# Low parts of 32 weight slabs by accumulating DMAs onto the negated rounded weights

## The chip, the cores and the metric

The kernel runs on one core of one Trainium2 chip, in one launch. The metric is the device time of that launch in microseconds (us), as a median of several executions. The engines of the core are TensorE (PE in the rows, with its weight loads as PEld), VectorE (DVE), ScalarE (ACT), GpSimd (POOL) and SyncE (SP), which here only issues DMAs.

## The reference, cut to what matters

One step of an encoder layer over 640 tokens (512 of a prompt, 128 of eight sample groups), width 1024:

```python
h = rmsnorm(x, norm_mix_g)
z = h @ w_in                      # query latent | kv latent | rotary key | GLU input | two gates
q = rmsnorm(c_q, q_norm_g) @ w_uq # then rotary, attention over cache and prompt -> attn_branch
u = u2[..., :C] * sigmoid(u2[..., C:])
conv_branch = silu(layernorm(depthwise_conv(u))) @ w_conv_out
x = x + (sigmoid(g_a) * attn_branch + sigmoid(g_c) * conv_branch) @ w_out
x = x + square(relu(rmsnorm(x) @ w_ff_up)) @ w_ff_down
x = x + sigmoid(rmsnorm(x) @ w_ple_gate) * (p_emb @ w_ple_proj)
```

All of it is float32. The products that this document is about are the query down-projection (`w_cq`), the query up-projection (`w_q`), the two gates (`w_gate`) and the projection of the convolution's branch (`w_conv_out`).

## The kernel before, in words

TensorE multiplies in float32r, a rounded form of float32. To keep the accuracy, each operand is split: a high part `hi` (the value rounded to float32r) and a low part `lo` (value minus `hi`). A product then has three terms, hi by hi, hi by lo and lo by hi, each for two halves of the 640 tokens: `mms` (L332) issues, for each block of 128 rows of the contraction, `wh*xh`, `wh*xl`, `wl*xh`, two matmuls each. So the low part of a weight slab is first read by the fifth matmul of its product. A product over 1024 rows has 48 matmuls, one over 768 rows (`w_q`) has 36.

Weights come as a stream of slabs (`jobs`, L224 to L254). `fetch` (L260) starts the load of the next slab into one of three buffers `raw` on SP's queue. `prep` (L269) takes a loaded slab, has ScalarE round it into `hi` (L287), and makes a function `low` that subtracts `hi` from `raw` into `lo` (L290), on VectorE, or on GpSimd for the slabs named in `POOL_SLABS` (L48: `w_gate` 0 to 7 and `w_q` 4 and 5). Then it calls `fetch` again. There are three buffers each for `hi` and `lo`. `slab` (L304) keeps three slabs ready, so the slab of product p+2 is prepared when the code comes to product p; its buffers are those of product p-1, and come free when TensorE has finished that product. `product` (L344) first runs the steps put down for the start, then issues some taps of the convolution, then `flush` (the `low` of the slab just prepared), then the matmuls, then the steps put down for after them.

The order of the instructions on each engine is the order of the code. Beside the products run: the convolution, three of its four channel tiles on VectorE (L485, the sums in PSUM), the fourth with multiplications on ScalarE (L501, L502) and additions on GpSimd (L510), two taps at most for each product; and short chains that make a norm's factor for each token. The one that matters here is that of the query latent, `chain("cbc")` (L744): for each of six products `cq`, ScalarE rounds the result (L363), VectorE makes its low part (L364), ScalarE squares it (L445), and GpSimd adds the squares (L446, `ssum_cq`). After the product `qr0` TensorE sums over partitions (L402, `ps_cbc`), VectorE scales (L641, L642), GpSimd takes the power (L643), VectorE multiplies (L644) and makes diagonal blocks (L419, `dg_cbc`), and after the product `qr1` TensorE spreads them (L395, `psb_cbc`). A like chain for the kv latent (`rkv`) stands earlier; between its steps VectorE has the rotary key (L699 to L702), whose multiplication waits for the load of `rope_k` (L695). That load is issued on SP behind the stores of the convolution's state (L624, L625), which go out in pieces of 120 bytes.

Products in order around the change: `kv0`, `kv1`, `kr`, `cq0` to `cq5`, `qr0`, `qr1`, `qn0` to `qn3` (the last six read `w_q` 0 to 5), `sc0` to `sc7` and `sa0` to `sa7` (`w_gate` 0 to 15), and eight products `co` on four slabs `w_conv_out`.

Of the kernel before, what the change touches and what calls it, by code (L numbers as in the profile page):

```python
# [14 lines left out]
P = 128  # L15
D = 1024
NP_ = 512          # prompt tokens
NB = 8             # sample batches
NQ = 16            # tokens per sample batch
NS = NB * NQ  # L20
T = NP_ + NS       # 640 columns: prompt tokens, then sample tokens (b, q)
# [6 lines left out]
C = 256            # latent width  # L28
QL = 768
CC = 512           # conv channels  # L30
# [9 lines left out]
# columns of the packed per-partition vectors  # L40
NT_RING = 9
SPLIT = 5  # the rows of the last product from here on by two groups of tokens: the norm of the first runs under the second
SO_LAG = 2.0
# taps of the convolution beside each product
# [3 lines left out]
POOL_SLABS = [f"w_gate_{i}" for i in range(8)] + ["w_q_4", "w_q_5"]  # L48
FFN_SLOPE, FFN_WAIT = 0.01, 0.2
POOL_LOW = (0, 1, 2, 3)  # of each four slabs of the lower product those whose second half Pool splits  # L50
# [7 lines left out]
NORM = ("DVE2", "DVE2", "ACT")  # of query tiles (3), (0, 1), (2): who divides by the sums of the softmax  # L58
# [4 lines left out]
SQ = ("M", "M", "M", "A")  # C11 C12 C21 C22: the square on the scalar engine alone, or the product on the vector engine  # L63
SQ2, START, SQ3 = "POOL", "POOL", "POOL"
UP_S = ("POOL", "POOL", "POOL", "DVE2")  # S1 S2 S3 S4
DN_S = ("POOL", "POOL", "POOL", "POOL")
DN_T = ("POOL", "DVE2", "POOL", "POOL")
UP_PS = (1, 0)  # the sums of weights in PSUM
# [4 lines left out]
FAST = (0, 1, 2, 3, 4, 5, 6)  # the chunks of the lower product by seven products  # L73
# the schedule of the attention: time between groups of samples, lag of the prompt, cost of a wait
# [6 lines left out]
class Slots:  # L81
    """Hands out tags of one-buffer slots; a freed slot goes to the back of the queue."""
# [17 lines left out]
class Plan:  # L100
    """A list schedule: operations with rough costs, issued in the order in which a model of the
    engines would start them. Engines, results waited for, and buffers taken and given back count."""
# [66 lines left out]
def encoder_step_kernel(ctx: ExitStack, tc: tile.TileContext, a: dict, o: dict):  # L169
# [7 lines left out]
    # PSUM by phase: two-bank tiles for the wide products (one of them for the sums of the  # L177
    # convolution), single banks for attention and what follows
# [81 lines left out]
    def fetch():  # L260
        """Starts the load of the next slab."""
        if pos[0] < len(jobs):
            src, cols, nm = jobs[pos[0]]
            pos[0] += 1
            raw = wraw.tile([P, 1024], F32, tag="raw", name=f"raw_{nm}")
            nc.sync.dma_start(raw[: src.shape[0], :cols], src)
            raws.append((raw, cols, nm))

    def prep():  # L269
# [4 lines left out]
        raw, cols, nm = raws.pop(0)  # L274
# [6 lines left out]
        if nm.startswith("cache_T"):  # L281
            # room for the new keys behind those of the cache
            hv, lv = (t.rearrange("p (c n) -> p c n", c=2)[:, :, :512] for t in (hi, lo))
            rv = raw.rearrange("p (c n) -> p c n", c=2)
        else:
            hv, lv, rv = hi[:, :cols], lo[:, :cols], raw[:, :cols]
        nc.scalar.activation(hv, rv, AF.Identity)  # L287

# [23 lines left out]
    # Each engine issues in the order of the code. Steps of a chain that wait for one another on  # L312
    # several engines are put between the products: `after` n products, or at the start of the nth next.
# [18 lines left out]
    def mms(ps, ws, xs, m=P, first=True, last=True):  # L332
        """ps[:m] += sum over k of w_k.T x_k with both operands split; ws: (hi, lo) blocks; xs: (hi, lo) [128, 640]."""
# [23 lines left out]
    def split(hi, lo, src, g=None):  # L357
        """hi + lo == src (times g) exactly, both in float32r."""
# [9 lines left out]
    def split_later(hi, lo, src, g=None):  # L368
        """split, the low part at the start of the next product."""
# [21 lines left out]
    def colsum(src, name):  # L391
        """Sum over partitions, on every partition."""
        ps = mm_ps(name)
        for s in range(2):
            nc.tensor.matmul(ps[:, s, :HT], ones, src[:, s * HT : (s + 1) * HT], start=True, stop=True)  # L395
        return ps

    def tok_sum(src, name):
        """Sum over partitions, tokens on partitions: [128, 5]."""
# [8 lines left out]
    def rstd(ssum, width, eps, name, which=0, out=None):  # L408
        """(ssum / width + eps) to the power, by token: [128, 5]."""
# [6 lines left out]
    def diag(r, name):  # L416
        """A column of tokens [128, 5] as five diagonal blocks; colsum makes it a row on every partition."""
# [13 lines left out]
    def sqsum(acc, src, first, name):  # L431
        """acc (+)= src * src."""
# [15 lines left out]
    def big(name):  # L448
        """[128, 8, 640] float32r pair as four slots."""
# [21 lines left out]
    def conv_ops():  # L471
        """The sums of the taps stay in PSUM: a multiply-add then leaves the port to GpSimd."""
# [22 lines left out]
    def conv_ops0():  # L495
        """The first channel tile: products on the scalar engine, sums on GpSimd."""
# [45 lines left out]
    # the first two slabs come in parts between the rows of x, so that the products start early  # L542
# [20 lines left out]
    # the clock of the tensor engine rises with use  # L563
# [64 lines left out]
    kv = Q.get([P, 4, T], "kv")  # raw 0:2, normalised 2:4  # L628
# [8 lines left out]
    def joint_rstd(ssum, width, name, scale, rc, rsq):  # L637
        """scale * rc * rsqrt(rc^2 * ssum / width + eps), by token: [128, 5]."""
# [8 lines left out]
    def chain(out, ssum, width, name, scale, then):  # L647
        """The row of joint_rstd by way of three products, then `then`."""
# [33 lines left out]
    def lat_new():  # L682
        """the new latents of the sample groups by token"""
# [30 lines left out]
    def rope_pair(xa, xb, n, name, out):  # L714
        """o1 = xa cos - xb sin, o2 = xb cos + xa sin; then out(o1, o2)."""
# [18 lines left out]
    cqA = [Q.get([P, 4, T], f"cq{i}", F32R) for i in range(3)]  # hi 0:4 | lo 0:4 | hi 4:6, lo 4:6  # L734
# [141 lines left out]
    krs = [t[:96, 2048:] for t in kTs]  # raw rotary keys of a group, three times  # L876
# [4 lines left out]
    # rotary parts, split and stacked: [hi hi lo] of the queries meets [hi lo hi] of the keys  # L881
# [65 lines left out]
    # slabs of the weight stream: k-th of the region takes the buffers of the (k - 3)rd  # L947
    slab_at, used = [], []

    def slab_op(key, hi_cost=0.95, lo_eng="DVE", lo_cost=1.14, raw_only=False):  # L950
        """Returns the index and the ops that complete the slab."""
# [30 lines left out]
    # keys and values of the prompt  # L982
# [54 lines left out]
    # absorbed queries of the sample groups  # L1037
    # the outputs of a group take the place of its queries
# [57 lines left out]
    # sample groups: scores, maximum, exponentials, transposes, values, back to latents on partitions  # L1096
# [3 lines left out]
    def group(b):  # L1100
# [14 lines left out]
        def key_new():  # L1115
            """the new keys of the group behind those of its cache"""
# [132 lines left out]
    # prompt: block-causal, query tiles of 128; a unit is a head with query tiles (3), (0, 1) or (2)  # L1249
    pair = {}  # L1250

    def unit(u, h, ts):
# [47 lines left out]
        # transposed blocks by key tile, the query tiles of one key tile side by side  # L1300
# [19 lines left out]
        def values():  # L1320
            """the outputs of a pair of heads share a bank"""
# [74 lines left out]
    # The channel mixer multiplies by one level of Strassen's method (Winograd's form): seven products  # L1396
    # of halves instead of eight. Rows in two halves by parity of their tile (B1x even, B2x odd), tokens
    # in two halves (Bx1, Bx2); of the operands B11, B21, B22, T1 = B12 - B11, T2 = B22 - T1,
    # T3 = B22 - B12, T4 = B21 - T2.
# [15 lines left out]
    def operand(i):  # L1415
        """Operand i as pairs (hi, lo) by pair of row tiles."""
# [11 lines left out]
    vrow = R.get([P, T], "vrow")  # mean(x^2) + eps of a token: r2 = 1 / v  # L1428
    ev2 = cols_[:, 4:9]  # eps v^2
# [22 lines left out]
    # the norm of the channel mixer by way of a column  # L1452
# [17 lines left out]
    def token_row(i, out, dep, key):  # L1470
        """A column of tokens as a row on every partition."""
# [27 lines left out]
    # the weight stream of the region  # L1499
    loads = []  # L1500

    def load(nm, key):
        """Starts the load of the next slab; its tile is in the box."""
# [28 lines left out]
    def take(cost, fn, deps, key):  # L1532
        """An op of the scalar engine that takes a pair of split buffers: they are taken in order."""
# [9 lines left out]
    def weights(nm, key):  # L1543
        """A slab for plain products, split; its pair of buffers is in the box."""
# [19 lines left out]
    # the values of the sample groups, from the outputs over the latents  # L1564
# [1238 lines left out]
```

## Time and profile before

| | us |
|---|---|
| median of 3 runs (1003.68 to 1004.9) | 1004.87 |
| span of the profiled execution | 1003.1 |
| TensorE busy in it | 977.9 |
| VectorE busy | 798.2 |
| ScalarE busy | 507.7 |
| GpSimd busy | 370.0 |

The profile is one execution; its span is 1.8 us below the median of the timed runs. Matmuls overlap one another: one takes some 0.31 us by its record, but in a product one starts every 0.147 us. A row of the timeline gives the start, the duration, the engine, the line, and what is written from what; in square brackets at its end stands how long the engine was idle before it and what ended that. Rows for several like instructions are merged (x2).

### The profile page before, as it was taken

The page shows a single profiled execution, that of the slowest core. Times are in us where ns is not written, and L with a number is a line of the kernel's source. Part 1 is how long each engine was busy: PE and PEld are TensorE (multiplying, and loading weights), DVE is VectorE, ACT ScalarE, POOL GpSimd, SP SyncE. Part 2 cuts the span into 40 slices and gives each one's busy share as a digit, 9 for nine tenths or more (in the row PEclk, how much of TensorE's full clock was granted, in tenths as well). Part 3 has the DMA queues.
Part 4 walks back from the last instruction along what each step waited for, and adds up shares of the span by engine and source line. Part 5 has one row for each costly group of instructions (what it writes and reads, how often), then busy time and mean ns, then how long its engine had stood idle before and what let it go on. Part 6 is the DMA issues. An engine that isn't in the chain of part 4 may idle for free.

```text
span 1003.1 us, 17048 instructions
## 1 busy us (share of the span) xinstructions
PE 977.9 (97%) x6570; PEld 941.1 (94%) x6570; DVE 798.2 (80%) x1417; ACT 507.7 (51%) x941; POOL 370.0 (37%) x270
## 2 busy tenths in 40 slices
PE   8999999999999999999999899999999999999996
PEld 8999989999999777799998799999999999999995
DVE  6596899995554787777888999999999999996445
ACT  7334544223443777635565445555455555645443
POOL 0354559322201433000329435454545454414011
PEclk9999999999999999999999999999999999999998
DMA  6329213312142343323312122223232222342203
GB/s 228 120 81 91 99 48 94 123 64 85 63 131 71 114 129 108 111 64 124 103 43 85 63 73 97 83 86 88 85 100 87 86 85 84 111 125 65 85 1 105
DMA packets 34705, 92.53 MB, mean 92 GB/s; under 512 B 8800, under 2 KB 11488, under 8 KB 34624
## 3 DMA queue, kind: packets, MB, share of 16 engines
q1 hardware_dynamic: 34480, 91.42, 30.7%
q8 instruction: 52, 0.85, 0.3%
q14 instruction: 29, 0.24, 0.1%
q10 hardware_dynamic: 144, 0.03, 0.0%
HBM read 86.12 MB, written 3.91 MB: 90 GB/s over the span
## 4 chain that ended last, share of the span: by engine, by line
PE 80%; DVE 12%; DMA 2%; ACT 2%; issue 2%; POOL 2%; SPq 0%; DVEq 0%; POOLq 0%; ACTq 0%
PE a L1909 10%; PE da L2176 9%; PE sa L342 6%; PE sc L342 6%; PE wo L1678 6%; PE b L1909 5%; PE db L2176 5%; PE pg L2472 3%; DVE cv L485 3%; PE ao L1615 3%; PE co L342 3%; PE pd L2292 3%; PE c L1909 2%; PE dc L2176 2%; PE pg L2551 2%; PE qn L342 2%
## 5 line engine op out<-in xcount | busy, mean ns | idle before, releaser
L2132 POOL TENSOR_TENSOR lo_B<-raw_down,hi_B 128x768 fp32r<-128x768 f32 x28 | 51.8, 1850 | 44.4 <-PE da L2176 21.1
L485 DVE SCALAR_TENSOR_TENSOR cv<-uP,keep,cv 128x512 f32<-128x512 f32 x87 | 65.6, 754 | 2.4
L2213 DVE TENSOR_TENSOR x<-da,x 128x320 f32<-128x320 f32 x112 | 53.7, 483 | 3.2 <-PE da L2176 0.9
L510 POOL TENSOR_TENSOR acc<-acc,tap 128x640 f32<-128x640 f32 x30 | 49.2, 1639 | 10.1 <-ACT tap L502 8.7
L2176 PE MATMUL da<-f,hi_B 128*128 128x320 f32 x224 | 50.2, 310 | 0.0
L2176 PE MATMUL da<-f,hi_A 128*128 128x320 f32 x224 | 49.6, 307 | 0.0
L2176 PE MATMUL db<-f,hi_A 128*128 128x320 f32 x224 | 49.6, 307 | 0.0
L1705 POOL TENSOR_TENSOR ssum<-ssum,sq 128x640 f32<-128x640 f32 x7 | 11.0, 1572 | 93.9 <-ACT sq L1702 93.9
L2113 POOL TENSOR_TENSOR raw_down<-raw_down 128x256 f32<-128x256 f32 x28 | 21.4, 763 | 60.5 <-DVE S L2105 60.1
L2125 ACT ACTIVATE hi_B<-raw_down 128x768 fp32r<-128x768 f32 x28 | 23.7, 848 | 31.4 <-PE a L1909 13.4
L1678 PE MATMUL wo<-mgl,hi_wo 128*128 128x320 f32 x128 | 39.4, 308 | 0.0
L1678 PE MATMUL wo<-mgh,hi_wo 128*128 128x320 f32 x128 | 39.1, 305 | 0.0
L1678 PE MATMUL wo<-mgh,lo_wo 128*128 128x320 f32 x128 | 39.0, 305 | 0.0
L2176 PEld LDWEIGHTS da<-f,hi_B 128*128 128x128 f32 x224 | 36.9, 187 | 0.7 <-DVE x L2213 0.2
L2176 PEld LDWEIGHTS db<-f,hi_A 128*128 128x128 f32 x224 | 37.1, 188 | 0.0
L2176 PEld LDWEIGHTS da<-f,hi_A 128*128 128x128 f32 x224 | 37.1, 188 | 0.0
L2125 ACT ACTIVATE hi_A<-S 128x512 fp32r<-128x512 f32 (+1 forms) x56 | 26.8, 479 | 17.4 <-DVE S L2119 17.4
L2176 PE MATMUL da<-f,lo_A 128*128 128x320 f32 x112 | 34.4, 307 | 0.8 <-DVE lo_A L2132 0.7
L2176 PE MATMUL db<-f,lo_A 128*128 128x320 f32 x112 | 34.2, 305 | 0.0
L2176 PE MATMUL da<-f,lo_B 128*128 128x320 f32 x112 | 34.2, 305 | 0.0
L2045 POOL TENSOR_TENSOR f<-y,f 128x640 fp32r<-128x640 f32 x7 | 11.7, 1673 | 59.7 <-ACT f L2038 59.7
L485 DVE SCALAR_TENSOR_TENSOR cv<-uS,keep,cv 128x128 f32<-128x128 f32 x87 | 31.0, 356 | 3.2
(686 smaller groups left out, 3785.5 us busy)
## 6 DMA issues: line engine op xcount, KB each, us to landing
raw_down<-in_w_down_dram SPq DMA_DIRECT2D x32, 512.0 KB, 3.6
raw_w_gate<-in_w_gate_dram SPq DMA_DIRECT2D x16, 512.0 KB, 3.5
raw_cache_T<-in_cache_T_dram SPq DMA_DIRECT2D x8, 512.0 KB, 3.6
raw_cache_V<-in_cache_V_dram SPq DMA_DIRECT2D x8, 512.0 KB, 3.5
raw_wo<-in_w_out_dram SPq DMA_DIRECT2D x8, 512.0 KB, 3.6
raw_pg<-in_w_pg_dram SPq DMA_DIRECT2D x8, 512.0 KB, 3.5
raw_w_glu<-in_w_glu_dram SPq DMA_DIRECT2D x6, 512.0 KB, 4.4
raw_w_cq<-in_w_cq_dram SPq DMA_DIRECT2D x6, 512.0 KB, 3.9
```

The costliest lines, as they stand in the source:

```text
L342: nc.tensor.matmul(ps[:m, s, :HT], w_, x_[:, s * HT : (s + 1) * HT], start=st_, stop=sp)
L485: nc.vector.scalar_tensor_tensor(out=outs[i] if j == W - 1 else sums[i], in0=src, scalar=wj, in1=sums[i], op0=ALU.mult, op1=ALU.add,)
L510: nc.gpsimd.tensor_tensor(out=acc[:, 0, :], in0=acc[:, 0, :], in1=t, op=ALU.add)
L1615: nc.tensor.matmul(ps[:, :HT], w_, x_[:, halves_[s]], start=k == 0 and n == 0, stop=k == 3 and n == 2)
L1678: nc.tensor.matmul(bx[s][:, :HT], w_, x_[:, n_], start=k == 0 and j == 0, stop=k == 7 and j == 2)
L1909: nc.tensor.matmul(bx[bank][:, :HT], w_, x_, start=first and k == 0 and i == 0, stop=k == 3 and i == 2, skip_group_check=True,)
L2125: nc.scalar.activation(bx[tile][0][:, dst], src(), AF.Identity)
L2132: eng.tensor_tensor(out=l_, in0=src(), in1=h_.bitcast(F32), op=ALU.subtract)
L2176: nc.tensor.matmul(bx[bank][:, :HT], w_, x_, start=first and n == 0 and i == 0, stop=n == 1 and i == 2, skip_group_check=True,)
L2213: nc.vector.tensor_tensor(out=d, in0=bx[bank][:, :HT], in1=d, op=ALU.add)
L2292: nc.tensor.matmul(ps[:, :HT], w_, x_, start=b_ == 0 and q_ == 0, stop=b_ == 3 and q_ == 2)
L2472: nc.tensor.matmul(bx[s][:, :HT], w_, x_[:, n_], start=k == 0 and i == 0, stop=k == 7 and i == 2)
```

## The change

The slabs of `w_cq` (6), `w_q` (6), `w_gate` (16) and `w_conv_out` (4) no longer get a `low`. In its place ScalarE writes the negated weights, rounded to float32r, into `lo`, and a DMA issued from GpSimd reads the slab from HBM a second time and adds it onto `lo`, which leaves weight minus rounded weight. Both stand in `prep`, right behind the rounding, and so ahead of the taps of the same product. `POOL_SLABS` has no more effect. The other lines of the diff take out comments.

```diff
+DMA_LOW = ("w_cq", "w_q", "w_gate", "w_conv_out")
...
-            raws.append((raw, cols, nm))
+            raws.append((raw, cols, nm, src))
...
-        raw, cols, nm = raws.pop(0)
+        raw, cols, nm, src = raws.pop(0)
...
         nc.scalar.activation(hv, rv, AF.Identity)
+        if nm.startswith(DMA_LOW):
+
+            nc.scalar.activation(lv, rv, AF.Identity, scale=-1.0)
+            nc.gpsimd.dma_start(lv, src, accum_op=ALU.add)
+            ready.append((hi, lo))
+            fetch()
+            return
 
         def low(eng=nc.gpsimd if nm in POOL_SLABS else nc.vector):
             eng.tensor_tensor(out=lv, in0=rv, in1=hv.bitcast(F32), op=ALU.subtract)
```

## Rows read from the trace of the kernel before

**Rows 1.** The page, its first part: busy time of each engine over the span.

```profile
PE 977.9 (97%) x6570; PEld 941.1 (94%) x6570; DVE 798.2 (80%) x1417; ACT 507.7 (51%) x941; POOL 370.0 (37%) x270
```

**Rows 2.** Busy time by stretch, the stretch that holds the change (first row: columns).

```profile
core 0: us, PE busy (x) PEld busy (x) DVE busy (x) ACT busy (x) POOL busy (x), PEclk, DMA share, GB/s
66.00:330.00 264.00, 261.64 (x1749) 256.12 (x1748) 195.91 (x280) 105.08 (x159) 99.67 (x65) 1.00 0.36 89
```

**Rows 3.** Who waited for whom, TensorE, 60 to 360 us: total, times, longest.

```profile
PE psb_cbc L395 <- DVE dg_cbc L419: 1.5, 1, 1.5
...
PE psb_rkv L395 <- DVE dg_rkv L419: 0.4, 1, 0.4
```

**Rows 4.** Timeline of TensorE around the chain of the query latent.

```profile
139.79 1.27 PE L402 MATMUL ps_cbc<-ones,ssum_cq 128*128 128x1 f32 x10 [0.43 <-POOL ssum_cq L446]
...
147.98 1.31 PE L395 MATMUL psb_cbc<-dg_cbc,ones 128*128 128x320 f32 x4 [1.53 <-DVE dg_cbc L419]
```

**Rows 5.** Chain of waits, 95 to 171 us: start, us, what.

```profile
134.41 2.09 DVE lo_w_q L290
...
137.39 0.71 ACT sqcq L445
...
138.17 1.57 POOL ssum_cq L446
...
141.50 1.59 POOL acc L510
...
144.26 1.19 POOL cbc L643
...
145.47 1.52 DVE cbc L644
...
147.01 0.84 DVE dg_cbc L419
```

**Rows 6.** Timeline of VectorE, the same stretch.

```profile
136.42 0.87 DVE L364 SCALAR_TENSOR_TENSOR cq<-cq,vec,cq 128x640 fp32r<-128x640 f32 x1
...
141.81 2.09 DVE L290 TENSOR_TENSOR lo_w_q<-raw_w_q,hi_w_q 128x768 fp32r<-128x768 f32 x1
143.82 0.15 DVE L641 SCALAR_TENSOR_TENSOR cbc<-ps_cbc,cols 128x5 f32<-128x5 f32 x1
```

**Rows 7.** Timeline of ScalarE, the last copy of the query latent and two roundings.

```profile
134.12 0.79 ACT L363 ACTIVATE cq<-cq,vec 128x640 fp32r<-128x640 f32 x1 [0.88 <-PE cq L342]
...
150.51 0.85 ACT L287 ACTIVATE hi_w_q<-raw_w_q 128x768 fp32r<-128x768 f32 x1
...
159.58 1.06 ACT L287 ACTIVATE hi_w_gate<-raw_w_gate 128x1024 fp32r<-128x1024 f32 x1 [3.52 <-PE qn L342]
```

**Rows 8.** Timeline of TensorE, the first low parts of `w_q` 4 and `w_gate` 0.

```profile
160.26 0.45 PE L342 MATMUL qn<-cq,lo_w_q 128*128 128x320 f32 x2
...
170.82 0.46 PE L342 MATMUL sc<-hTh,lo_w_gate 128*128 128x320 f32 x2
```

**Rows 9.** The tile `raw_w_gate`: its load, a subtraction on GpSimd (ns min/median/max), landing.

```profile
L266 SPq DMA_DIRECT2D raw_w_gate<-in_w_gate_dram x16: 327/328/514, 149.8 to 245.7; - x16
...
L290 POOL TENSOR_TENSOR lo_w_gate<-raw_w_gate,hi_w_gate x8: 2400/2404/2417, 165.2 to 208.3; 128x1024 fp32r<-128x1024 f32 x8
...
DMA to landing us min/median/max: 3.3/3.5/4.9
```

**Rows 10.** DMA issues of the page and of 76 to 100 us: KB each, us to landing.

```profile
raw_w_q<-in_w_q_dram SPq DMA_DIRECT2D x6, 384.0 KB, 3.0
...
uS<-in_conv_hist_dram SPq DMA_DIRECT2D x1, 736.0 KB, 5.7
...
out_conv_s_dram<-uS SPq DMA_DIRECT2D x1, 480.0 KB, 17.9
keep<-in_rope_k_dram SPq DMA_DIRECT2D x1, 80.0 KB, 17.4
```

**Rows 11.** Busy time by stretches of 2 us, columns as in the second group.

```profile
82.00:84.00 2.00, 2.00 (x16) 1.83 (x15) 1.93 (x4) 1.91 (x3) 0.60 (x1) 1.00 1.70 43
...
94.00:96.00 2.00, 2.00 (x16) 2.00 (x15) 0.35 (x1) 0.00 (x0) 0.02 (x1) 1.00 0.79 268
```

**Rows 12.** Timeline of VectorE, the rotary key's multiplication.

```profile
95.65 0.81 DVE L702 TENSOR_TENSOR krb<-krb,keep 32x640 f32<-32x640 f32 x1 [2.42 <-DMA keep<-in_rope_k_dram]
```

## The prediction, made before the result was known

> **What bounds the kernel now.** I read the page's busy times first: TensorE is busy for 977.9 of 1003.1 us, so no other engine bounds the whole [rows 1]. Then the busy time of the stretch that holds the 32 slabs, 66 to 330 us. TensorE works for 261.64 of its 264 us, at a granted clock of 1.00, the upper level of 2.4 GHz [rows 2]. The change takes no matmul away, so all that it can win there is the idle 264 - 261.64 = 2.36 us. The waits of TensorE say where this is: 1.5 us for `dg_cbc` and 0.4 us for `dg_rkv` [rows 3], and in the timeline 0.43 us for `ssum_cq` ahead of `ps_cbc`; the exact size of the first is 1.53 us [rows 4]. These three make 2.36 us. VectorE is busy for 195.91 us of the stretch, ScalarE for 105.08, GpSimd for 99.67 [rows 2]: work that leaves VectorE or GpSimd is worth only what it does for those three waits.
>
> **What leaves, and what that is worth.** 22 subtractions leave VectorE and 10 leave GpSimd (2.4 us each there [rows 9]). Most stand beside matmuls and ended no wait. Three of them matter, in the chain of the query latent. The chain of waits shows `lo_w_q` on VectorE for 2.09 us, right ahead of the low part of the last `cq`, which then starts at 136.42; behind it come the square (137.39), `ssum_cq` (138.17, 1.57 us) and TensorE's sum [rows 5, 6]. ScalarE's copy, the other thing that the low part needs, ends at 134.12 + 0.79 = 134.91 [rows 7]. Without the subtraction the low part starts at about 134.95, that is 1.47 us earlier, and `ssum_cq` ends at 138.17 + 1.57 - 1.47 = 138.27. TensorE is there at 139.79 - 0.43 = 139.36 [rows 4]. So the wait of 0.43 us goes.
>
> The second part: VectorE then has taps and another `lo_w_q` (2.09 us from 141.81), and only behind it L641 at 143.82 [rows 6]. Both edits bring L641 to about 140.7, where the result of `ps_cbc` is the later one (139.36 + 1.27 = 140.63 [rows 4]). What is late next is GpSimd, whose queue holds, ahead of the power: `ssum_cq`, the new DMA of `w_q` 2, and two additions of taps of 1.59 us [rows 5]. The DMA waits for ScalarE: square from 135.92, rounding and negation of 0.85 us each [rows 7], so until about 138.3. GpSimd's time to issue it stands in no row; I take 1.2 us, the row of GpSimd's smallest arithmetic instruction here (1.19 us for 5 columns [rows 5]), with bounds of 0.33 us (SP's issue) and 2.4 us (the subtraction that it replaces) [rows 9]. Then the power runs from 138.3 + 1.2 + 3.2 = 142.7 to 143.9. In the row it ran from 144.26 to 145.45. L644 took 1.52 us beside an addition on GpSimd [rows 5], the like L641 0.15 us [rows 6]; behind the power there now stands a DMA, so I take 0.15 us. With the diagonal's 0.84 us the blocks are done at about 145.0 (146.3 if L644 stays at 1.52 us, about the same if the issue takes 2.4 us). TensorE arrives at 147.98 - 1.53 - 0.43 = 146.02. So this wait goes too. Together 0.43 + 1.53 = **1.96 us won**, with bounds of 1.5 and 1.96.
>
> **What is added on ScalarE.** 32 negations, of the same form as the roundings (1.06 us for 1024 columns, 0.85 for 768 [rows 7]): 26 x 1.06 + 6 x 0.85 = 32.7 us. ScalarE is busy for 105.08 of 264 us [rows 2]; queued behind each are the taps of its product, which feed only GpSimd. I cost it at nothing, beyond its place in the chains above and below.
>
> **What is added on GpSimd and in the DMA engines.** 32 DMAs that GpSimd issues. The profile of before has none such. Behind each, while it waits for the negation, queue the additions of taps, of squares, and the powers; that was worked out for the one chain that is near a wait. The two rotary products of the queries (L719) move back by some 2 us; what they make is first read by the attention, behind 330 us.
>
> The question for each slab is whether its low part lands before TensorE reads it. The time for it is from the end of the negation to the fifth matmul of the product. The tightest is `w_q` 4: rounding ends at 150.51 + 0.85, negation at 152.21, first use at 160.26 [rows 7, 8]: 8.05 us. `w_gate` 0: 159.58 + 1.06 + 1.06 = 161.70 to 170.82, 9.12 us [rows 7, 8]. The others have 9 to 13 us by the same reckoning, and those behind a late VectorE get more when its subtractions leave.
>
> Against it stands issue plus landing. Plain loads land in 3.5 us for 512 KB and 3.0 us for 384 KB [rows 9, 10], 0.5 us for 128 KB. An accumulating DMA reads the slab and the tile and writes the tile: by 1024 KB moved 3.5 + 2.0 = 5.5 us, by 1536 KB 7.5 us; for 384 KB 4.5 or 6.0 us. With 1.2 us of issue 6.7 to 8.7 us against 9.1 and more, and 5.7 to 7.2 us against 8.05. The upper bound is a DMA that shares its engines with the stores of the convolution's state: a 480 KB store took 17.9 us [rows 10]. I take the first set, as the load of 736 KB in 5.7 us [rows 10] lies nearest; so I cost it at nothing, and its cover is the 8.05 us.
>
> The Trainium skill ("Collectives: The Full Stack", section "The bandwidth ceiling: the fold count and why AG ≠ RS ≠ AR") states that an add within the DMA engines costs no cycles of its own but needs two source reads, which halves the rate; with "DMA: Bandwidth & Descriptors", section "Anatomy of one DMA — SWDGE (gpsimd) path", some 2.0 us plus bytes at 436 GB/s, that would make an estimated 2.0 + 2 x 1.2 = 4.4 us for a slab, less than the 5.5 us above, and the wait would be as absent. No run here shows either yet.
>
> **The load of `rope_k`.** It lands 17.4 us after its issue, behind the stores of small pieces (17.9 us) [rows 10], and VectorE idles 2.42 us for it [rows 12]; the 0.40 us of TensorE's wait for `dg_rkv` hang on it, and every further us of it is one of TensorE's. The accumulating DMAs of `w_cq` 0 and 1 fall into just this time. Lower bound nothing: at 82 to 84 us the engines move 43 GB/s, at 94 to 96 us 268 GB/s [rows 11], so bytes are not what they lack. Upper bound: two DMAs at their whole data time, 1024 KB each at 0.5 us for 128 KB, 2 x 4.0 = 8.0 us. Between: the store has 4096 pieces in 17.9 us, 4.4 ns each; the two DMAs have 2 x 128 rows with two reads, 512 pieces, 2.2 us. The engines have 1.70 transfers open at a time [rows 11], so I let half be hidden: **1.1 us lost**.
>
> **Sum.** -1.96 + 1.1 = -0.9 us on the profiled span of 1003.1 us, and the same on the median: 1004.9 - 0.9 = **1004.0 us**. What a measurement can tell from no change is 0.2%, 2.0 us. More HBM traffic (26 x 512 + 6 x 384 KB = 15.6 MB on 23.5 MB, 148 GB/s in place of 89 [rows 2]) costs nothing beside the 268 GB/s of [rows 11].
>
> **Rivals.** *Low parts that land late* (slower). The mechanism decides from 8.05 us of issue and landing on. From there a slab's way sets the pace: in a stage of 48 matmuls its buffer comes free two products (14.1 us) before the start of the product, and it needs some 2.5 us until ScalarE is there, 2.1 us of rounding and negation, and x for issue and landing, against 14.1 + 0.6 us. Each us of x over 10 is half a us a product: x = 12 gives 32 x 1.0 = 32 us (1037 us), x = 10.5 some 8 us (1013 us). For: nothing in the trace shows such a DMA's speed. Against: the 5.7 us for 736 KB. *`rope_k` costs its data time*: 2.2 to 8.0 us, thus 1005.1 to 1010.9 us. For it speaks the Trainium skill, "DMA: Bandwidth & Descriptors", section "Queues, rings and completion order": an engine takes its queues in turn, packet by packet, so the new packets are served ahead of the store's tail; the traces show no two queues at work yet. *`rope_k` costs nothing*: 1004.9 - 1.96 = 1002.9 us, with the 0.40 us for `dg_rkv` left. *No relief*: issuing holds GpSimd as long as the subtraction did, or L644 stays slow and more stands ahead of the power; then the waits of the chain stay and 1.1 us is lost: 1006 us.
>
> **How the numbers follow.** Forecast (both waits of the chain gone, about 1 us for `rope_k`) 0.38; nothing for `rope_k` 0.16; data time for `rope_k` 0.14; late low parts 0.24; no relief 0.08. The range goes from 1002.5 (all 2.36 us won) to 1016 (the near half of the late cases); beyond it lie 0.12 of the late ones and 0.06 below. Faster by more than 2.0 us: half of the second case and a little of the first, 0.14; slower by more: the late cases, two thirds of the third, half of the last, 0.37; the rest 0.49.
>
> **What would show it.** Right: `ps_cbc` and `psb_cbc` start without a wait, TensorE's wait for `dg_rkv` is near 1.5 us, and no wait of TensorE names a low part. Wrong: TensorE waits for DMAs onto `lo_w_cq`, `lo_w_q` or `lo_w_gate`; issue and landing above 8 us; a clock below 1.00 in the stretch; GpSimd held for over 2.4 us by an issue.

## The result, and the profile after

The changed kernel took 1010.19 us (median; 1009.47 to 1010.36) beside 1004.87 us for the kernel before on the same chip: a ratio of 1.0064, 95% interval 1.0050 to 1.0078. It is slower, by some 0.6%. On another chip, with more runs, it was 1008.35 us beside 1003.63 us: 1.0050, 1.0034 to 1.0066. Of the first 5.3 us the profiled executions show 4.6 (span 1007.7 us against 1003.1 us).

The page's busy times, and the stretch that holds the 32 slabs:

```profile
PE 979.0 (97%) x6570; PEld 942.2 (94%) x6570; DVE 766.3 (76%) x1395; ACT 536.7 (53%) x973; POOL 369.3 (37%) x292
```

```profile
core 0: us, PE busy (x) PEld busy (x) DVE busy (x) ACT busy (x) POOL busy (x), PEclk, DMA share, GB/s
66.00:330.00 264.00, 257.91 (x1726) 253.40 (x1724) 159.77 (x250) 131.18 (x186) 98.56 (x85) 0.99 0.69 146
```

The offload itself did what it says. Against [rows 1, 2] VectorE is relieved of 36 us in the stretch, ScalarE carries 26 us more, GpSimd has its time. But TensorE idles 264 - 257.91 = 6.09 us there, where it idled 2.36 us before. Its waits (total, times, longest), to be held against [rows 3]:

```profile
PE cq L350 <- DMA lo_w_cq<-in_w_cq_dram: 4.3, 1, 4.3
PE psb_cbc L403 <- DVE dg_cbc L427: 1.4, 1, 1.4
PE ps_mu L403 <- DVE lnsum L815: 0.3, 1, 0.3
```

The short waits for `ssum_cq` and `dg_rkv` are gone. The wait for `dg_cbc` (1.4 us) stands where it stood. Two are new, and one is large: TensorE waits for the low part of `w_cq` 0. In TensorE's timeline (start, duration):

```profile
89.51 0.45 PE L350 MATMUL cq<-hTl,hi_w_cq 128*128 128x320 f32 x2
94.31 0.90 PE L350 MATMUL cq<-hTh,lo_w_cq 128*128 128x320 f32 x2 [4.35 <-DMA lo_w_cq<-in_w_cq_dram]
95.01 0.73 PE L350 MATMUL cq<-hTh,hi_w_cq 128*128 128x320 f32 x2
```

The second and third rows also show matmuls that last longer than the first: two took 0.90 and 0.73 us, where two take 0.45 at the upper level. Windows of 2 us give the clock (span, TensorE busy, granted clock, DMA share, GB/s):

```profile
88.00:90.00 2.00, 1.96 (x16) 1.00 1.80 108
90.00:92.00 2.00, 0.00 (x0) 0.70 0.96 135
92.00:94.00 2.00, 0.00 (x0) 0.50 1.13 214
94.00:96.00 2.00, 1.69 (x6) 0.50 0.99 196
96.00:98.00 2.00, 2.00 (x11) 0.59 1.02 372
98.00:100.00 2.00, 2.00 (x15) 1.00 1.07 274
```

While TensorE stood still, the clock fell to 0.50, the lower level (1.2 GHz), and was back at 1.00 only behind 98 us, after TensorE had worked again for over 3 us. So one late slab is paid twice: 4.35 us of wait and some 1.6 us of slow matmuls. From the first matmul of `cq` to `psb_rkv` the kernel before needed 97.34 - 89.66 = 7.68 us, the changed one 102.36 - 89.13 = 13.23 us: 5.55 us more (4.35 + 1.6, less the 0.40 us of the wait for `dg_rkv`, which now lies in their shadow).

Read from the timelines of TensorE, the start of the first matmul of a tile, after minus before, in us:

```
first matmul of   cq     psb_rkv  ps_cbc  psb_cbc  ps_mu   kn      sx      da      pd
at (before)       89.66  97.34    139.79  147.98   233.59  314.28  341.88  569.72  888.68
after - before    -0.53  +5.02    +4.34   +4.13    +4.63   +4.71   +3.18   +4.32   +4.09
```

So the whole loss arises in one product. Between `kn` (314 us) and the end nothing is lost on balance; the ups and downs there are taken up below.

Why the slab was late is in the DMA issues of the stretch 70 to 100 us (KB each, median us from issue to landing) and in the tile's own answer (landing min, median, max over the six slabs of `w_cq`; 16.4 us is slab 0):

```profile
raw_w_cq<-in_w_cq_dram SPq DMA_DIRECT2D x4, 512.0 KB, 13.7
lo_w_cq<-in_w_cq_dram POOLq DMA_DIRECT2D x3, 512.0 KB, 13.4
out_conv_s_dram<-uS SPq DMA_DIRECT2D x1, 480.0 KB, 20.3
keep<-in_rope_k_dram SPq DMA_DIRECT2D x1, 80.0 KB, 19.9
```

```profile
L292 POOL DMA_DIRECT2D lo_w_cq<-in_w_cq_dram x6: 856/877/1064, 77.9 to 122.6; - x6
...
DMA to landing us min/median/max: 7.0/8.7/16.4
```

GpSimd issued it at 77.90, right behind SyncE's store of the convolution's state (issued at 76.93, 480 KB in pieces of 120 bytes, 20.3 us). It landed at 94.3; TensorE had come for it at 89.96. `w_cq` 1 and 2 took 13.4 and 9.9 us, and TensorE, late by then, didn't wait for them. The other low parts landed in time: 7.0 to 7.5 us for the last three of `w_cq`, 5.1 to 7.8 us for the six of `w_q`, 6.0 to 8.9 us for the sixteen of `w_gate`, 6.1 to 8.8 us for the four of `w_conv_out`.

### The profile page after: what moved, and what is told of

Read it like the earlier page. It is cut to its first block, busy times and chain, and to the rows that moved or that the text cites. A ratio compares the mean times of both kernels' runs of the same rounds, so it can differ in the third digit from the quotient of the medians.

```text
span 1007.7 us, 17119 instructions
## 1 busy us (share of the span) xinstructions
PE 979.0 (97%) x6570; PEld 942.2 (94%) x6570; DVE 766.3 (76%) x1395; ACT 536.7 (53%) x973; POOL 369.3 (37%) x292
## 4 chain that ended last, share of the span: by engine, by line
PE 85%; DVE 6%; POOL 3%; DMA 2%; ACT 2%; issue 2%; SPq 0%; DVEq 0%; POOLq 0%; ACTq 0%
PE a L1917 10%; PE da L2184 9%; PE sc L350 6%; PE sa L350 6%; PE wo L1686 6%; PE b L1917 5%; PE db L2184 4%; PE pg L2480 3%; PE ao L1623 3%; PE co L350 3%; PE pd L2300 3%; PE glu_b L350 2%; PE glu_a L350 2%; PE c L1917 2%; PE dc L2184 2%; PE cq L350 2%
## 5 line engine op out<-in xcount | busy, mean ns | idle before, releaser
L292 POOL DMA_DIRECT2D lo_w_gate<-in_w_gate_dram x16 | 13.9, 872 | 74.7 <-ACT lo_w_gate L291 74.7
```

## The experiments

The letters A and B are set anew in each expectation. Through most of them, A is the theory that the loss lies at one place, the early slabs beside the small stores; B blames the accumulating DMAs themselves, as the first that GpSimd issues (e1, e2, e5) or wherever they run (e8). Profiles stand for single executions; medians are from several. A ratio is taken over the runs, and can differ a little from that of the two medians.

**One slab, or two, back on VectorE.**

```
-        if nm.startswith(DMA_LOW):
+        if nm.startswith(DMA_LOW) and nm != "w_cq_0":                    # e1
+        if nm.startswith(DMA_LOW) and nm not in ("w_cq_0", "w_cq_1"):    # e8
```

> The changed kernel, but the low part of w_cq 0 alone is subtracted on VectorE again; 31 accumulating DMAs stay. Theory A: the DMA of w_cq 0 (16.4 us to landing) was late because it shares the DMA engines with the 4608 small pieces of the convolution's state stores. Then TensorE's wait of 4.35 us and the 1.6 us at the lower clock behind it go; the DMA of w_cq 1, still within the stores, stays at some 13 us and costs at most 1 us of wait, the load of rope_k at most 2 us: span 1007.7 - 5.95 + 1 to 3 = 1003 to 1005 us. Theory B: the first DMA that GpSimd issues is slow by itself. Then w_cq 1 inherits 16.4 us, lands at about 101 us and TensorE waits some 3.7 us for it: span 1005.5 to 1007.

> The changed kernel, but the low parts of w_cq 0 and w_cq 1, whose DMAs fall into the small stores, are subtracted on VectorE; 30 accumulating DMAs stay, the stores are as they were. Theory A (only DMAs beside the stores are late): TensorE waits for no low part, the load of rope_k lands in 17 to 18 us as before; against the kernel before 0.4 us (ssum_cq) are won and 0.3 us (ps_mu) lost: ratio 0.999 to 1.001. Theory B (accumulating DMAs cost TensorE elsewhere too): ratio above 1.002.

With `w_cq` 0 on VectorE the loss at `psb_rkv` turned from +5.02 to -0.87 us against before, and what was left is the next slab:

```profile
PE cq L350 <- DMA lo_w_cq<-in_w_cq_dram: 0.6, 1, 0.6
```

With both on VectorE no wait for a low part is left. TensorE's waits of 66 to 330 us are then:

```profile
PE psb_cbc L403 <- DVE dg_cbc L427: 1.4, 1, 1.4
PE ps_mu L403 <- DVE lnsum L815: 0.3, 1, 0.3
```

At `psb_rkv` e8 is 1.70 us ahead of before, 1.14 us of which it had at the start of `cq`, so the 0.40 us for `dg_rkv` went and nothing was lost. From there to `kn` run its 30 accumulating DMAs, and it gains another 0.29 us: on balance they cost TensorE nothing up to 312 us. Medians: e1 1005.71 against 1003.13 us (1.0026, 1.0013 to 1.0039), e8 1005.74 against 1003.24 us (1.0032, 1.0020 to 1.0044). This is less than the change's loss, but not zero, though e8 stands 1.99 us ahead at `kn`; by the bound that its expectation set (1.002) it is theory B's case. Where that goes is the last question of this section.

**The stores taken away as a suspect.** e2 copies the state into a tile on ScalarE, and stores it from there in 512 whole pieces. e5 moves the small stores (of 4096 pieces, and 512 more for `conv_p`) behind `w_cq`, beside the slabs of `w_q`.

```
-    start(2, lambda: nc.sync.dma_start(o["conv_s"], uS[:, :, :, NQ:]))
+    nc.scalar.activation(t[:, :480]..., uS[:, ct, :, NQ:], AF.Copy)        # e2, two halves
+    nc.sync.dma_start(o["conv_s"][:, ct], t[:, :480]...)
+    start(10, lambda: nc.sync.dma_start(o["conv_s"], uS[:, :, :, NQ:]))    # e5
```

> The changed kernel with all 32 accumulating DMAs, but the convolution's state is first copied by ScalarE (four copies) into two contiguous tiles, and stored in 512 pieces of 240 and 1920 bytes, not 4608 of 120. Theory A (the stores make the first accumulating DMAs late): those of w_cq 0 and 1 land in 7 to 9 us as the others do, TensorE waits for no low part and its clock stays at 1.00, rope_k lands within 8 us; the wait of 1.4 us for dg_cbc stays: span 1007.7 - 5.95 = 1001.8 us, some 0.2% below the kernel before. Theory B (the first DMA of GpSimd is slow): w_cq 0 stays at 13 to 16 us, the wait of 4.3 us stays, span 1007 to 1008.

> The changed kernel with the small stores of the convolution's state issued eight products later, at the start of qr0 (about 134 us) in place of kv1. Theory A (the stores make accumulating DMAs late): the wait for the low part of w_cq 0 and the lower clock at 91 to 97 us go, its DMA lands in 7 to 9 us; the DMAs issued from 138 to 150 us (w_q 2, w_q 3) now take 12 to 17 us where 8 to 10 are there, so TensorE waits 2 to 7 us for a low part of w_q, or for a rounding behind a late load. Theory B (the first DMA of GpSimd is slow): the wait of 4.3 us at cq0 stays.

In e2 the DMA issues of the same stretch read:

```profile
lo_w_cq<-in_w_cq_dram POOLq DMA_DIRECT2D x3, 512.0 KB, 7.2
out_conv_s_dram<-state SPq DMA_DIRECT2D x2, 240.0 KB, 4.2
keep<-in_rope_k_dram SPq DMA_DIRECT2D x1, 80.0 KB, 5.8
```

The same accumulating DMAs, the same bytes of state, and the slabs land in 7.2 instead of 13.4 us (medians of three): no wait for a low part, the clock at 1.00. e2 took 1002.89 us against 1003.13 us (0.9999, 0.9987 to 1.0012). In e5 the stall moves with the stores: `cq` runs through (-0.97 us at `cq`, -1.53 at `psb_rkv`), and TensorE waits for a slab of `w_q` instead. Its timeline, the landings of `lo_w_q` and the windows of 2 us say so:

```profile
149.60 0.70 PE L350 MATMUL qn<-cq,lo_w_q 128*128 128x320 f32 x2 [2.14 <-DMA lo_w_q<-in_w_q_dram]
```

```profile
DMA to landing us min/median/max: 5.2/7.6/12.8
```

```profile
148.00:150.00 2.00, 0.40 (x2) 0.96 1.00 256
150.00:152.00 2.00, 2.00 (x10) 0.50 0.98 278
152.00:154.00 2.00, 2.00 (x11) 0.68 1.06 300
```

From -2.42 us at `psb_cbc` to +1.53 us at `sc`, this stall cost 3.95 us: 2.14 of wait, the rest at the lower clock. So the cause is the small stores, not the place of `w_cq`. Nor is it that a DMA is GpSimd's first: in e5 none of `w_cq` took over 8.3 us.

**Is it the adding?** e4 lets the same DMAs copy the slab in place of adding it, so its products are made with whole weights where the low parts belong.

```
-            nc.gpsimd.dma_start(lv, src, accum_op=ALU.add)
+            nc.gpsimd.dma_start(lv, src)
```

> The changed kernel, with the 32 DMAs of GpSimd as plain copies of the slab in place of accumulations, so that the subtraction is left out and the low parts hold the weights themselves; the time alone counts. If the accumulation's further traffic makes the landing (7.8 us for a slab of w_gate), it falls to 4.4 to 5.5 us (3.5 us of a plain load and 0.9 us of issue). If the way by GpSimd is what costs, it stays at 7 to 8 us. For w_cq 0, within the state stores: with the smaller traffic 8 to 13 us in place of 16.4, TensorE's wait 0 to 1 us and the span 1002 to 1004; if its turns with the stores are what it waits for, it stays near 16 us with the wait of 4.3 us.

Adding has a price, and it is not the price of the stall. The landings of `lo_w_gate` (512 KB), first in e4, then in the changed kernel:

```profile
DMA to landing us min/median/max: 4.4/4.6/6.5
```

```profile
DMA to landing us min/median/max: 6.0/7.8/8.9
```

For `w_q` it is 3.9 against 6.1 us. But `w_cq` 0 landed after 17.0 us as a plain copy too, and TensorE waited 5.0 us for it (1008.38 us, one execution). How the store makes it late, the packets of the queues show (packets, MB, share of 16 engines' time; q0 is GpSimd's queue, q1 SyncE's). In the changed kernel, from the issue at 77.9 us to 85 us, and then from 85 to 90 us:

```profile
q1 hardware_dynamic: 3390, 0.66, 153.4%
```

```profile
q0 software_dynamic: 93, 0.38, 90.7%
q1 hardware_dynamic: 667, 0.08, 71.3%
```

For over 7 us no row of the slab moved at all, while 3325 packets under 512 bytes went by SyncE's queue; then 93 of the slab's 128 rows took 5 us. In e2 the first row moved 2.1 us after the issue, and between 80.4 and 85 us all 128 were through:

```profile
q0 software_dynamic: 143, 0.52, 69.6%
```

So the slab is held twice: its rows start late, and then they go slowly beside what is left of the store. Why the first row starts so late, no row shows.

The Trainium skill ("DMA: Bandwidth & Descriptors", section "Queues, rings and completion order") says that an engine takes its queues in turn, and drains a whole packet of several descriptors from one before it switches. That a queue of few large rows doesn't pass one of many small pieces, the runs show (16.4 us beside the small stores, 7.2 beside whole ones); the turn itself they can't test, as no row shows which pieces make up such a packet, and the 7 us in which the slab stood still it doesn't explain. For the adding, the estimate of 4.4 us that the prediction worked out from two pages of the Trainium skill ("Collectives: The Full Stack" and "DMA: Bandwidth & Descriptors") is too low: 7.8 us was measured, and 4.6 for the copy alone.

**The wait that stayed.** e3 takes the tap's addition away from GpSimd behind the power of the query norm.

```
-QR_TAPS = (4, 1)
+QR_TAPS = (5, 0)
```

> The changed kernel with the taps beside qr0 and qr1 as (5, 0) in place of (4, 1): no addition of a tap stands on GpSimd behind the power of the chain cbc. Theory A: VectorE's product of that chain (2.47 us in the changed kernel, ending with GpSimd's addition) is held by this addition; then it takes under 1 us, the wait of 1.42 us ahead of psb_cbc goes, span 1006.3 us. Theory B: it is held by GpSimd's issuing of the DMA: it takes 0.9 to 1.5 us and ends with the issue, the wait is under 0.3 us. Theory C: it is slow by itself: 2.4 us and the wait stay, span 1007.7.

The chain of the query norm in the changed kernel, VectorE and GpSimd, and then in e3:

```profile
147.41 1.20 POOL L651 TENSOR_TENSOR cbc<-cbc,cols 128x5 f32<-128x5 f32 x1
148.57 0.91 POOL L292 DMA_DIRECT2D lo_w_q<-in_w_q_dram  x1
149.24 1.84 POOL L518 TENSOR_TENSOR acc<-acc,tap 128x640 f32<-128x640 f32 x1
...
148.64 2.47 DVE L652 SCALAR_TENSOR_TENSOR cbc<-cbc,cols 128x5 f32<-128x5 f32 x1 [2.81 <-POOL cbc L651]
```

```profile
148.22 1.20 POOL L651 TENSOR_TENSOR cbc<-cbc,cols 128x5 f32<-128x5 f32 x1
149.39 0.92 POOL L292 DMA_DIRECT2D lo_w_q<-in_w_q_dram  x1
...
149.45 0.17 DVE L652 SCALAR_TENSOR_TENSOR cbc<-cbc,cols 128x5 f32<-128x5 f32 x1 [1.31 <-POOL cbc L651]
```

L652 writes five columns. It takes 2.47 us and ends, at 151.11, with GpSimd's addition (151.08); with the addition gone it takes 0.17 us, although the issue of a DMA runs on GpSimd at the same time. So here an issue didn't hold VectorE's instruction, and an addition did. The rows of GpSimd overlap (148.57 + 0.91 is past 149.24), so when exactly the addition began is not to be read. In e3 the wait for `dg_cbc` is gone, and `psb_cbc` starts 1.80 us nearer to before than `ps_cbc`; the stall at `cq` stays (4.5 us), and with it the loss: 1009.52 against 1003.13 us (1.0064, 1.0039 to 1.0089; the four runs lie between 1007.11 and 1012.68 us, and the profiled one, with its span of 1005.3 us, is the fastest).

**Both edits, with the DMAs and without.** e6 has the whole stores and the moved tap on the changed kernel, e7 the same two edits on the kernel before; e10 and e11 are the same two kernels once more on another chip, beside e9, the changed kernel itself, and e12, the kernel before with whole stores alone.

> The changed kernel with the state stored in whole pieces and the taps (5, 0), the two edits that took away its two waits. From the spans: 1007.7 - 5.95 (wait for w_cq 0 and lower clock) - 1.4 (dg_cbc) = 1000.3 us, against 1003.1 for the kernel before; ratio to it 0.996 to 0.999. TensorE then waits in the stretch of 66 to 330 us only 0.3 us, ahead of ps_mu.

> The kernel before, without any accumulating DMA, with the same two edits (state stored in whole pieces, taps (5, 0)). Theory A: the accumulating DMAs themselves win the wait of 0.43 us for ssum_cq and hardly more; then this kernel comes within 0.1% of the one with both edits and the DMAs: the wait for dg_rkv (0.4 us) goes, that for dg_cbc falls from 1.53 us to under 0.5 as the VectorE product no longer meets an addition; ratio to the kernel before 0.997 to 0.999. Theory B: without the subtractions on VectorE much more is won: it stays at the kernel before, 0.2% or more above the version with the DMAs.

> The changed kernel as it is, for a second profile and a median of more runs. So far its TensorE stands 4.7 us behind the kernel before at the first matmul of kn (314 us) and 5.3 us behind at the end by the medians. Theory S (what the change does lies whole in 66 to 330 us; what differs behind it are two chance events, the clock's fall at about 335 us, 1.4 us, and the sum of the down weights that falls behind a GpSimd subtraction at about 868 us, 2 to 3 us): the wait for lo_w_cq is 4 to 5 us again, kn stands 4.0 to 5.2 us behind, and the times spread over 3 to 4 us about a ratio of 1.004 to 1.007. Theory P (the accumulating DMAs leave something behind that costs 1 to 2 us beyond 330 us in every run): the same wait, and the difference behind 330 us is on the side of a loss in this profile too.

> The kernel with the accumulating DMAs, the state stored in whole pieces and no tap addition on GpSimd beside the power, once more. Its first profile had both chance events (1.4 us at 335 us, 2.3 us at 868 us) and stood 0.3 us behind its twin without DMAs at kn, but 4.2 us at 888 us. Theory S: at kn within 0.6 us of its twin again, and at least one of the two events is missing in this profile, or present in the twin's. Theory P: both events are there again, and both are missing in the twin; the median is 1.5 us or more above the twin's, as it was (2.2 us).

> The twin of the kernel above without the DMAs, once more. Its first profile had neither event. Theory S: kn at 311.8 us again, and one of the two events present in about half of such profiles; the median within 1 us of the kernel above. Theory P: neither event, median 1.5 us or more below the kernel above.

> The kernel before with only the state stored in whole pieces. Both theories: no wait for rope_k on VectorE, which the small stores delayed, and PE no earlier than the kernel before by more than 0.5 us at kn, since that wait of 2.42 us was covered: 1002 to 1004 us, ratio 0.999 to 1.001. With the DMAs and whole stores the median was 1002.89 us on another chip against 1003.13 us before; Theory P: this kernel is 1 to 2 us below the kernel before, as nothing else of the DMAs is left in it.

```
                                    median us   before us   ratio (95%)               at kn, us from before
e9   changed kernel                 1008.35     1003.63     1.0050 (1.0034-1.0066)    +4.78
e6   both edits, DMAs               1004.27     1003.24     1.0013 (1.0004-1.0021)    -2.20
e10  the same again                 1003.01     1003.63     1.0002 (0.9991-1.0012)    -2.50
e7   both edits, no DMAs            1002.08     1003.24     0.9991 (0.9982-1.0000)    -2.52
e11  the same again                 1002.90     1003.63     0.9990 (0.9980-0.9999)    -2.63
e12  whole stores, no DMAs          1003.70     1003.63     1.0003 (0.9993-1.0012)    -1.43
```

e9 repeats the changed kernel's stall (3.7 us, landed late beside a store of 19.4 us) and its place at `kn`. With both edits, the kernel with DMAs stands 0.1 to 0.3 us behind the one without at 314 us. Its two waits there, in e10:

```profile
PE ps_mu L403 <- DVE lnsum L823: 0.3, 1, 0.3
PE co L350 <- DMA lo_w_conv_out<-in_w_conv_out_dram: 0.3, 1, 0.3
```

So, freed of the stores, 32 accumulating DMAs are a draw up to 314 us: the two edits win most of what can be won there without them. The forecast for e6 (0.996 to 0.999) was missed on both chips, and e7 and its repeat e11 came within 0.1% of the same edits with the DMAs on one chip of two; e12 came out as forecast by its median, but stood 1.43 us ahead at `kn` (0.78 us of it at `cq` already) where at most 0.5 was expected. e7 is the fastest version made, at the edge of what its interval can tell from no change.

**What lies behind 314 us.** The code there is the same in all kernels, yet the profiles differ by up to 4 us in how far they fall back. Three places hold most of this. One, of up to 1.3 us, lies between `c` and `da` (518 to 570 us; the changed kernel lost 1.27 us there, e9 nothing) and wasn't followed further. Another is the clock at the start of the attention: after two waits of 1.5 us together it fell in the profiles of before, e6 and e12, and in no other, which is worth 1.5 us. (So from 342 us on a profile without it shows 1.5 us too much gain over that of before.) The waits are the same in e10, the same kernel as e6. The windows of 334 to 342 us, of e6 and of e10 (span, TensorE busy and its matmuls, granted clock, DMA share, GB/s):

```profile
334.00:342.00 8.00, 7.24 (x38) 0.79 0.24 79
```

```profile
334.00:342.00 8.00, 7.55 (x53) 1.00 0.43 135
```

The third is in the feed-forward layer, at about 868 us: a sum on VectorE that waits for a load of the down weights either runs just before GpSimd's subtraction `lo_B`, or falls behind it and is held. First e7, then e10:

```profile
866.08 0.42 DVE L2113 TENSOR_TENSOR S<-raw_down 128x256 f32<-128x256 f32 x1
...
866.48 1.85 POOL L2140 TENSOR_TENSOR lo_B<-raw_down,hi_B 128x768 fp32r<-128x768 f32 x1 [2.98 <-PE db L2184]
```

```profile
865.72 1.85 POOL L2148 TENSOR_TENSOR lo_B<-raw_down,hi_B 128x768 fp32r<-128x768 f32 x1 [2.98 <-PE db L2192]
...
866.43 1.43 DVE L2121 TENSOR_TENSOR S<-raw_down 128x256 f32<-128x256 f32 x1 [1.03 <-DMA raw_down<-in_w_down_dram]
```

It cost e10 1.9 us between `da` and `pd` (-4.22 to -2.32), e6 2.3, e8 1.8, e1 2.3 and e2 3.3. The margin in e7 is 0.40 us, less than the spread of that load's landing (3.4 to 4.8 us).

Theory S (chance events) was right on the event at 335 us: the twins e6 and e10 differ in it, and the medians of the last two, e10 and e11, are 0.1 us apart. It was not borne out on the one at 868 us: all five profiles of kernels with accumulating DMAs and no stall of over 1 us have it (e1, e2, e6, e8, e10), and none of the four without these DMAs (before, e7, e11, e12) nor of the five with a stall (after, e3, e4, e5, e9).

One row of the trace goes with the event. Near this load every profile has one packet of 8 KB in queue 14, which the profile calls `instruction`, and its place differs from kernel to kernel. In the five profiles with the event it started 3.1 to 3.7 us after the load was issued, and the load took 4.2 to 4.9 us. In e3, where it started 3.2 us after the issue, the load took 3.8 us. In the other eight it came ahead of the issue or over 4.4 us behind it, and the load took 3.5 to 3.7 us. In e10, whose load was issued at 861.5 us, the packet stands in the window of 864.9 to 865.3 us (packets, MB, share of time); below it the load's issue and landing:

```profile
q14 instruction: 1, 0.01, 4.8%
...
raw_down<-in_w_down_dram SPq DMA_DIRECT2D x1, 512.0 KB, 4.9
```

The same load in e7, whose packet went at 862.0 us, just ahead of the issue:

```profile
raw_down<-in_w_down_dram SPq DMA_DIRECT2D x1, 512.0 KB, 3.6
```

So a packet beside the load, and not the DMAs of 270 us themselves, is the likely reason that the load is late; no run moved the packet alone, and what sets its place no row shows. Whether the DMAs cost something behind 314 us thus stays open: by the medians it is 2.2 us on one chip and 0.1 us on the other.

## Why the prediction was wrong, point by point

The forecast was 1004.0 us, with no change as the likeliest outcome; the time was 1010.19 us, inside the range, on the side that had a chance of 0.37.

- **The step that failed: the landing of `w_cq` 0, costed at nothing.** The prediction had the number. It named the DMA that shares its engines with the state's stores as the upper bound, 17.9 us [rows 10], and then took one landing for all 32 slabs, by the nearest row. Slab 0 was issued 1 us behind the store: 0.32 us until GpSimd took it up (77.90) and 16.4 us from there to its landing, against the 12.4 us from the end of its negation (77.58) to TensorE's arrival (89.96). The bound was right within 1.5 us for just the slabs that it was about. Price: 5.55 us up to `psb_rkv`, against 1.1. A nearer row than the load of 736 KB stood in the trace of before: two plain loads of `w_cq`, 512 KB each, issued at 84.82 and 86.09 us behind the same store on SyncE's queue, took 11.3 us each, beside a cover of 12.4 us. The landings of `raw_w_cq` in the kernel before (min, median, max):

```profile
DMA to landing us min/median/max: 3.4/3.9/11.3
```

- **The term of 1.1 us for `rope_k` had the right neighbours and the wrong victim.** The DMAs of `w_cq` 0 and 1 do slow that load (19.9 us in place of 17.4 [rows 10]), but its 2 us lie in the shadow of the stall, and without the DMAs of these two slabs (e8) it landed in 16.1 us. What TensorE paid for was the store's hold on the slab, not the slab's on this load.
- **The clock is a part that the sum didn't have.** A wait of 4.35 us took the clock to 0.50, some 1.6 us more; in e5 2.14 us of wait cost 3.95 us.
- **The wait for `ssum_cq`: right.** It is gone, and from the first matmul of `qr` to `ps_cbc` 0.59 us were won (0.43 forecast).
- **The wait for `dg_cbc`: wrong by one term.** GpSimd's chain came as worked out: the power ran at 147.41 - 4.34 = 143.07 on before's time, 142.7 forecast. Mis-sized was L652, 0.15 us taken and 2.47 us measured. The DMA does stand behind the power, but its issue is short (0.91 us) and a tap's addition comes right behind. So 1.4 of the 1.53 us [rows 4] stayed. e3 shows the term: 0.17 us without the addition.
- **Landings elsewhere: right.** A landing is counted from the start of the issue (77.90 + 16.4 = 94.3, when TensorE went on), so the 7.8 us for 512 KB hold 0.87 us of issue (1.2 forecast) and lie inside 6.7 to 8.7; the 6.1 us for 384 KB lie inside 5.7 to 7.2. These are medians; the longest, 8.9 and 7.8 us, lie just beyond. No slab of `w_q` or `w_gate` made TensorE wait, so the rival of low parts that land late as a steady pace didn't come about: it came once, for one slab.
- **ScalarE's negations at nothing: right** up to the slabs themselves; no wait of TensorE names one.
- **GpSimd's queue was followed for one chain only.** Another was near a wait: `lnsum` (L813) stands behind a DMA that waits for its negation, and ran at 235.32 where it ran at 210.69 before. TensorE waits 0.32 us for what follows from it. GpSimd's timeline (idle time ahead, and who ended it):

```profile
234.76 0.86 POOL L292 DMA_DIRECT2D lo_w_gate<-in_w_gate_dram  x1 [6.18 <-ACT lo_w_gate L291]
235.32 1.90 POOL L813 TENSOR_TENSOR lnsum<-acc 128x640 f32<-128x640 f32 x1
```

- **The rivals.** `rope_k` at its data time had 1005.1 to 1010.9 us, which holds the time, by another mechanism. None said that one slab alone, beside the stores, would be late. And the new packets weren't served ahead of the store's tail, as the rival reckoned: the slab's rows stood still for over 7 us.

## What to carry to other kernels

Cost a moved transfer at the place where it will run: if one row shows a transfer of 18 us there, that row and not the nearest in size is its price, and the work that it feeds must have that much time. Here a store in small pieces delayed the transfers beside it in its own queue and in another (SyncE's loads of `w_cq` 13.7 us in place of 4.1 with whole pieces, GpSimd's DMAs 13.4 in place of 7.2), so collect such a store into whole pieces before putting more on the DMA engines. Where one engine's idle time bounds nothing, relieving it wins only the waits that it ends, and another edit (here the stores and one tap) may win the same for less.

## What the runs showed of the hardware

- An accumulating DMA of 512 KB from HBM onto a tile landed in 7.8 us (median), a plain one by the same queue in 4.6 us; for 384 KB 6.1 and 3.9 us. GpSimd spent 0.87 us on issuing it, and 0.55 us on the plain one.
- Beside a store of 4096 pieces of 120 bytes, a slab of 128 rows of 4 KB by GpSimd's queue took 16.4 us, and 17.0 us as a plain copy; with the state stored in 512 larger pieces 7.2 us. Its first row moved over 7 us after the issue, and 2.1 us with the larger pieces.
- A VectorE instruction on five columns took 0.17 us beside GpSimd's issue of a DMA, and 2.47 us beside GpSimd's addition of 640 columns.
- After 4.35 us without a matmul the clock stood at the lower level (0.50) for the first 3 us of work behind it; in e5 a wait of 2.14 us was followed by 0.50 too.
- A load of 512 KB landed after 4.2 to 4.9 us in five profiles in which a packet of the `instruction` queue started 3.1 to 3.7 us after its issue, and after 3.5 to 3.7 us in the eight in which this packet lay elsewhere (one, with 3.8 us, stands between).
